# A decoder trunk on one core: the first norm's weight as one row, and a written order for the first projection

## The chip, the cores and the metric

One core of a Trainium2 chip runs the whole program. The metric is the device time of one execution in microseconds (us); lower is better. TensorE (PE), VectorE (DVE), ScalarE (ACT), GpSimd (POOL) and SyncE (SP) each run their own list of instructions in order; SP issues nearly all the transfers (DMA).

## What is computed

Two layers on 256 tokens of width 1024, in float32. Layer 0 has stick-breaking heads and differential heads side by side, layer 1 has sparse attention, and each is followed by a squared-ReLU MLP. Every sub-layer starts with an RMS norm:

```python
def rmsnorm(x, g):
    x32 = x.astype(jnp.float32)
    y = x32 * lax.rsqrt(jnp.mean(x32 * x32, axis=-1, keepdims=True) + RMS_EPS)
    return (y * g.astype(jnp.float32)).astype(x.dtype)

proj = h @ w_in                       # h = rmsnorm(x, attn_norm[0])
sb_q, sb_k, sb_v, df_q, df_k, df_v = jnp.split(proj, 6, axis=-1)
```

The change concerns the very first of these norms and the projection `sb_v` behind it.

## The kernel before

The 256 tokens are two halves of 128 rows (`t` = 0 and 1), one token to a partition, 1024 columns in two parts of 512 (`n`). Matrix products need the width on the partitions, so a normed half (tile `xg`) is transposed by PE in pieces of 128x128 into `ps_t`, four to a PSUM bank.

To keep float32 accuracy at the fast product type, every operand is the sum of a high and a low part: the high part is a cast on ACT (`x0h` of the activations, `wh` of the weights), the low part is what the cast lost, a subtraction on DVE (`x0l`, `wl`). Each product is then three: high with high, low with high, high with low.

The class `Weights` streams the matrices. One entry of its list is 1 MB and comes in two loads of 512 KB (tile `w`, `load`, L48, issued by SP); `split` (L56) casts and subtracts each half. There are four load buffers (`RAW`), so the fifth load waits until DVE or POOL has read the first. The first entry is `sbv` 0 (rows 0 to 511 of the `sb_v` columns), the second `sbv` 1 (rows 512 to 1023), then `sbq` 0, `sbk` 0 and so on. For `sbv` 1 the subtraction is on POOL (`ON_POOL`, L38).

`run` (L1059) starts with the loads of x for token half 0 (two of 256 KB), the norm's weight, three weight halves, x for token half 1, a fourth weight half. `load_gain` (L243) brings the norm's weight to all partitions by a DMA that reads one row 128 times (512 KB). `identities` runs 13 products on zeros on PE ahead of the real work (`ps_warm`). `norm_full` (L297) then squares on ACT (L253), multiplies x by -0.5 and the weight on DVE (L294), forms the reciprocal root from logarithm and exponential on ACT and two small DVE operations (L258), multiplies `xg` by it (L309) and transposes. `constants` (L124) prepares small matrices on POOL and casts four of them on DVE. The first projection is `project_v` (L492): for token half 0 and then for token half 1, 24 products of 128x512 each. Behind it `halves` computes q and k of the first heads (`ps_f`, two entries, 96 products of 128x256), and then come the attention scores `z`.

The order of the instructions of an engine is set by a scheduler that places them when the program is built, from the order of the code; nothing pins it here.

Of the kernel before, what the change touches and what calls it, by code (L numbers as in the profile page):

```python
# [22 lines left out]
KT = D // P  # L23
EPS = 1e-6
# [8 lines left out]
class Weights:  # L33
# [1 line left out]


    RAW, SPLIT, BUFS = 4, 1, 4
    ON_POOL = [("sbv", 1)]  # L38

    def __init__(self, nc, pool):  # L40
        self.nc, self.pool = nc, pool
# [12 lines left out]
        self.raw.append(w)  # L54

    def split(self):  # L56
        i = len(self.ready)
        a, b = self.todo[i][1].shape[1:]
        n = a * b
        wh, wl = (self.pool.tile([P, 2048], F32R, tag=k, name=f"{k}{i}", bufs=self.BUFS) for k in ("wh", "wl"))  # L60
        for j in range(2):
            while len(self.raw) <= 2 * i + j:
                self.load()
            w = self.raw[2 * i + j]
            c = slice(j * n // 2, (j + 1) * n // 2)
            self.nc.scalar.copy(wh[:, c], w)  # L66
            key = self.todo[i][0]
            eng = self.nc.gpsimd if key in self.ON_POOL else self.nc.vector
            eng.tensor_sub(wl[:, c], w, wh[:, c].bitcast(F32))  # L69
        self.ready.append(tuple(t[:, :n].rearrange("p (a b) -> p a b", b=b) for t in (wh, wl)))  # L70

    def prefetch(self):
        while len(self.ready) < min(self.n_used + self.SPLIT + 1, len(self.todo)):
# [12 lines left out]
class Trunk:  # L86
# [18 lines left out]
        return self.psum.tile([P, 512], F32, tag="B", name=name, bufs=4)  # L105

    def mm(self, out, lhsT, rhs, start, stop, **kw):
        self.nc.tensor.matmul(out, lhsT, rhs, start=start, stop=stop, **kw)  # L108


    def identities(self):
        nc, c = self.nc, self.const
        self.ident = c.tile([P, P], F32, name="ident")
        make_identity(nc, self.ident)
        self.identb = c.tile([P, P], BF16, name="identb")
        nc.vector.tensor_copy(self.identb, self.ident)

        zero = c.tile([P, 512], BF16, name="zero")
        nc.vector.memset(zero, 0.0)
        ps = self.bankB("ps_warm")  # L120
        for i in range(13):
            self.mm(ps, zero[:, :P], zero, i == 0, i == 12)

    def constants(self):  # L124
        nc, c = self.nc, self.const

        u = c.tile([P, P], F32, name="u")
        nc.gpsimd.memset(u, -1.0)
        nc.gpsimd.affine_select(out=u, in_=u, pattern=[[-1, P]], compare_op=ALU.is_ge,
                                fill=0.0, base=0, channel_multiplier=1)  # L130
        self.negU = c.tile([P, P], F32R, name="negU")
        nc.vector.tensor_copy(self.negU, u)
        n1 = c.tile([P, P], F32, name="n1")
        nc.gpsimd.memset(n1, -1.0)
        self.neg1 = c.tile([P, P], F32R, name="neg1")
        nc.vector.tensor_copy(self.neg1, n1)

        m = c.tile([P, P], F32, name="m")
        nc.gpsimd.memset(m, 0.0)
        nc.gpsimd.affine_select(out=m, in_=m, pattern=[[1, P]], compare_op=ALU.is_gt,  # L140
                                fill=NEG, base=0, channel_multiplier=-1)
        self.maskb = c.tile([P, P], BF16, name="maskb")
        nc.vector.tensor_copy(self.maskb, m)
# [98 lines left out]

    def load_gain(self, row):  # L243
        self.gain = self.tmp.tile([P, D], F32, tag="gain", name="gain")
        self.nc.sync.dma_start(self.gain, row.partition_broadcast(P))

    def square_half(self, t, n):

# [6 lines left out]
        self.v = v  # L255
        return v

    def rsqrt(self, v):  # L258
# [3 lines left out]
        nc.scalar.activation(u, v, AF.Ln)  # L262
        nc.scalar.activation(y, u, AF.Exp, scale=-0.5)
        if v.shape[1] == 1:
            nc.vector.scalar_tensor_tensor(o, y, y, v, op0=ALU.mult, op1=ALU.mult)
        else:
            nc.vector.tensor_mul(o, y, y)
            nc.vector.tensor_mul(o, o, v)
        nc.vector.scalar_tensor_tensor(r, o, -3.0, y, op0=ALU.add, op1=ALU.mult)
        return r  # L270

    def split_psum(self, hi, lo, src):
# [214 lines left out]
    def even_mixer(self, xT, oT, pool, out):  # L487
        nc = self.nc
        vsb = pool.tile([P, 2, 512], F32, name="vsb")
        vdf = pool.tile([P, 2, 512], F32, name="vdf")  # L490

        def project_v(key, dst, between=None):  # L492
            w = [self.W.get((key, 0)), None]
            pss = [self.bankB("ps_v0"), self.bankB("ps_v1")]
            self.tmajor(pss[0], w[0], xT, 0, range(4), True, False)
            w[1] = self.W.get((key, 1))
            self.tmajor(pss[0], w[1], xT, 0, range(4, 8), False, True)
            nc.scalar.copy(dst[:, 0, :], pss[0])
# [20 lines left out]
        project_v("sbv", vsb)  # L519
# [539 lines left out]
    def run(self):  # L1059
        nc, a, tc = self.nc, self.a, self.tc  # L1060
        self.rs2 = {}
        self.x = self.const.tile([P, 2, D], F32, name="x")
        self.late = []
        self.weight_order()
        nc.scalar.preload_act_table_set("natural_log_exp_and_others")
        for n in range(2):
            nc.sync.dma_start(self.x[:, 0, n * 512 : n * 512 + 512], a["x"][0][:P, n * 512 : n * 512 + 512])
        self.load_gain(a["attn_norm"][0])
        for _ in range(3):
            self.W.load()  # L1070
        nc.sync.dma_start(self.x[:, 1, :], a["x"][0][P:, :])
        self.W.load()
        self.identities()
        xT = self.new_T("x0")
        for t in range(2):
            for n in range(2):
                self.norm_full(t, n, xT)
            if t == 0:
                self.W.split()
        self.constants()  # L1080
# [90 lines left out]
```

## Time and profile before

| | |
|---|---|
| median of 3 runs | 662.26 us (661.87 to 663.5) |
| profiled execution, its own time | 662.43 us |
| its span | 660.7 us |
| PE busy | 641.3 us, 97% of the span |
| DVE, ACT, POOL busy | 62%, 52%, 7% |
| chain that ended last: PE, DVE, ACT | 90%, 5%, 2% |
| moved by DMA | 108.67 MB, 164 GB/s over the span |

The span runs from the first to the last instruction that the profiler saw. "Busy" means that an engine executed something; PE works on products, and idle time of an engine that nobody waits for costs nothing. The chain that ended last is followed backwards from the last instruction, each time to what released it, so its pieces add up to the span.

### The profile page before, as it was taken

The numbers are of one execution on the slowest core, as the hardware profiler recorded it, in microseconds if no ns is written. First come the engines' busy times: TensorE is split into PE (matmuls) and PEld (weight loads), VectorE is DVE, ScalarE is ACT, GpSimd is POOL, SyncE is SP. The second block draws the span as 40 slices with busy tenths as digits, with TensorE's granted clock in tenths as the row PEclk, the third lists the DMA queues.
The fourth block names the chain that finished last, engine by engine and source line by source line (L and its number), as shares of the span: only waits on it lengthen the run. The fifth ranks groups of instructions, "written<-read, shape, count | busy, mean of one in ns | idle before, by whom it ended". The sixth has DMA issues, their size and how long they took to land.

```text
span 660.7 us, 11136 instructions
## 1 busy us (share of the span) xinstructions
PE 641.3 (97%) x4257; PEld 562.2 (85%) x4257; DVE 407.7 (62%) x820; ACT 345.5 (52%) x699; POOL 46.3 (7%) x139
## 2 busy tenths in 40 slices
PE   6999999999999999999999899999999999999995
PEld 3799898899898989988899778777899898999984
DVE  4845577886555555555877476776765555555534
ACT  5564666464444444543567374654554444444523
POOL 2200000000000000000203231440000000000000
PEclk8899999999999999999999999999999999999999
DMA  6785243456565556664596612014365555555501
GB/s 253 226 257 157 73 176 106 156 183 208 178 182 182 186 188 192 191 191 141 173 307 208 223 64 64 23 43 156 118 214 186 182 183 181 188 189 189 192 2 64
DMA packets 74277, 108.67 MB, mean 164 GB/s; under 512 B 5072, under 2 KB 60400, under 8 KB 74224
## 3 DMA queue, kind: packets, MB, share of 16 engines
q1 hardware_dynamic: 74224, 107.97, 50.9%
q8 instruction: 33, 0.54, 0.3%
q14 instruction: 20, 0.16, 0.1%
HBM read 106.91 MB, written 1.05 MB: 163 GB/s over the span
## 4 chain that ended last, share of the span: by engine, by line
PE 90%; DVE 5%; ACT 2%; issue 1%; DMA 1%; SPq 0%; ACTq 0%; DVEq 0%
PE macc L108 27%; PE ps_up L108 24%; PE ps_f L108 7%; PE acc L108 5%; PE ps_q L108 4%; PE ps_ut L108 3%; PE ps_v L108 2%; PE o L108 2%; PE s L108 2%; PE ps_or L108 2%; PE ps_k L108 2%; PE pt L1026 2%; DVE wl L69 2%; PE z L108 1%; PE ps_h L108 1%
## 5 line engine op out<-in xcount | busy, mean ns | idle before, releaser
L69 DVE TENSOR_TENSOR wl<-w,wh 128x1024 fp32r<-128x1024 f32 (+1 forms) x188 | 224.9, 1214 | 166.1 <-ACT wh L66 165.6
L66 ACT CAST wh<-w 128x1024 fp32r<-128x1024 f32 (+1 forms) x190 | 192.9, 1040 | 172.7 <-PE macc L108 83.3
L108 PE MATMUL macc<-wh,l 128*128 128x512 f32 x256 | 101.2, 395 | 0.0
L108 PE MATMUL macc<-wh,h 128*128 128x512 f32 x256 | 101.1, 395 | 0.0
L108 PE MATMUL macc<-wl,h 128*128 128x512 f32 x256 | 101.0, 394 | 0.0
L108 PE MATMUL ps_up<-m0h,wh 128*128 128x256 f32 x224 | 63.5, 283 | 0.0
L108 PE MATMUL ps_up<-m1h,wh 128*128 128x256 f32 x224 | 63.5, 283 | 0.0
L108 PE MATMUL ps_up<-m0h,wl 128*128 128x256 f32 x224 | 63.4, 283 | 0.0
L108 PE MATMUL ps_up<-m1h,wl 128*128 128x256 f32 x224 | 63.3, 283 | 0.0
L108 PE MATMUL ps_up<-m1l,wh 128*128 128x256 f32 x224 | 63.3, 283 | 0.0
L108 PE MATMUL ps_up<-m0l,wh 128*128 128x256 f32 x224 | 63.3, 283 | 0.0
L108 PEld LDWEIGHTS macc<-wh,l 128*128 128x128 f32 x256 | 48.2, 188 | 11.1
L108 PEld LDWEIGHTS macc<-wh,h 128*128 128x128 f32 x256 | 48.4, 189 | 10.0
L108 PEld LDWEIGHTS macc<-wl,h 128*128 128x128 f32 x256 | 48.3, 189 | 10.0
L108 PEld LDWEIGHTS ps_up<-m0l,wh 128*128 128x128 f32 x224 | 42.9, 191 | 0.6
L108 PEld LDWEIGHTS ps_up<-m1l,wh 128*128 128x128 f32 x224 | 42.9, 191 | 0.6
L108 PEld LDWEIGHTS ps_up<-m1h,wh 128*128 128x128 f32 x224 | 42.9, 191 | 0.6
L108 PEld LDWEIGHTS ps_up<-m0h,wh 128*128 128x128 f32 x224 | 42.9, 191 | 0.6
L108 PEld LDWEIGHTS ps_up<-m1h,wl 128*128 128x128 f32 x224 | 42.9, 191 | 0.0
L108 PEld LDWEIGHTS ps_up<-m0h,wl 128*128 128x128 f32 x224 | 42.9, 191 | 0.0
L983 POOL TENSOR_SCALAR p<-p,sums 128x128 f32<-128x128 f32 (+1 forms) x64 | 31.4, 508 | 80.5 <-ACT kd L720 25.8
L108 PE MATMUL ps_f<-x0h,wh 128*128 128x256 f32 x128 | 36.5, 285 | 0.0
(285 smaller groups left out, 1191.2 us busy)
## 6 DMA issues: line engine op xcount, KB each, us to landing
w<-in_mlp_w_dram SPq DMA_DIRECT2D x128, 512.0 KB, 4.3
w<-in_ev_w_in_dram SPq DMA_DIRECT2D x24, 512.0 KB, 4.8
w<-in_od_w_in_dram SPq DMA_DIRECT2D x18, 512.0 KB, 5.0
w<-in_ev_w_out_dram SPq DMA_DIRECT2D x8, 512.0 KB, 4.3
w<-in_od_w_out_dram SPq DMA_DIRECT2D x8, 512.0 KB, 3.6
cwk<-in_od_cmp_k_w_dram SPq DMA_DIRECT2D x8, 256.0 KB, 6.5
cwv<-in_od_cmp_v_w_dram SPq DMA_DIRECT2D x8, 256.0 KB, 5.1
w<-in_od_w_in_dram SPq DMA_DIRECT2D x4, 304.0 KB, 2.9
```

The costliest lines, as they stand in the source:

```text
L66: self.nc.scalar.copy(wh[:, c], w)
L69: eng.tensor_sub(wl[:, c], w, wh[:, c].bitcast(F32))
L108: self.nc.tensor.matmul(out, lhsT, rhs, start=start, stop=stop, **kw)
L983: nc.gpsimd.tensor_scalar(o[:, h], o[:, h], sums[:, h : h + 1], 0.0, op0=ALU.mult, op1=ALU.add)
L1026: nc.tensor.transpose(pt[:, h * P : (h + 1) * P], p[g, t, b][:, h, kt * P : (kt + 1) * P], self.ident)
```

## The change

In words, with the lines of the changed code:

- The weight of the first norm is loaded as one row of 4 KB into one partition (`g1`), by a DMA that ACT issues. PE multiplies it by a column of -0.5 in full float32 (`ps_g`, two products of 128x512 with one row of contraction), so that every partition has -0.5 times the weight in PSUM. One DVE pass then makes `xg` = x times reciprocal root times `ps_g`; the separate scaling pass is gone.
- SP loads in this order: x of token half 0, both halves of `sbv` 0, x of token half 1, both halves of `sbv` 1. The small loads of `scalars` (`lam`, `subln`) come behind the two halves of `sbq` 0, and the second norm's weight (`in_mlp_norm`) later, among the `ev_w_out` loads.
- 5 products on zeros in place of 13: four ahead of `ps_g`, one behind.
- For `sbv` 1 the high part is cast on POOL and the low part subtracted on DVE. The four casts of `constants` move from DVE to POOL, and one memset (`n1`) from POOL to DVE.
- A new function, `entry`, writes out the order of the norm and the projection for all engines and pins it; the order behind it is that of before apart from the rows that moved.

The core of the diff:

```diff
-    ON_POOL = [("sbv", 1)]
...
+    def hi(self, j, on_pool=False):
+        w, h, _ = self.half(j)
+        return (self.nc.gpsimd.tensor_copy if on_pool else self.nc.scalar.copy)(h, w)
+
+    def lo(self, j, i=None):
+        w, h, l = self.half(j, i)
+        return self.nc.vector.tensor_sub(l, w, h.bitcast(F32))
...
+        g1 = self.tmp.tile([1, D], F32, tag="xg", name="g1")
+        nc.scalar.dma_start(g1, self.a["attn_norm"][0].rearrange("(o d) -> o d", o=1))
+        nc.scalar.preload_act_table_set("natural_log_exp_and_others")
+        for n in range(2):
+            nc.sync.dma_start(self.x[:, 0, n * 512 : n * 512 + 512], self.a["x"][0][:P, n * 512 : n * 512 + 512])
+        W.open()
+        nc.sync.dma_start(self.x[:, 1, :], self.a["x"][0][P:, :])
+        for _ in range(2):
+            W.load()
+        self.identities()
...
+        self.warm(4)
+        for n in range(2):
+            keep(self.mm(ps_g[n], self.n1[:1, :], g1[:, n * 512 : n * 512 + 512], True, True))
+        self.warm(1)
...
+        def scale(t, r):
+            self.xg = self.tmp.tile([P, D], F32, tag="xg", name="xg")
+            for n in range(2):
+                c = slice(n * 512, n * 512 + 512)
+                keep(nc.vector.scalar_tensor_tensor(self.xg[:, c], self.x[:, t, c], r, ps_g[n], op0=ALU.mult,
+                                                    op1=ALU.mult))
...
+        square(0, 0)
+        square(0, 1)
+        scale(0, rs(0))
+        self.constants()
+        keep(W.hi(0))
+        keep(W.hi(1))
+        h, l0 = flip(0, 0)
+        keep(nc.scalar.copy(*h))
+        h, l1 = flip(0, 1)
+        square(1, 0)
+        keep(nc.scalar.copy(*h))
+        square(1, 1)
+        keep(W.lo(0))
+        keep(nc.vector.tensor_sub(*l0))
+        keep(W.lo(1))
+        keep(nc.vector.tensor_sub(*l1))
+        W.close()
+        scale(1, rs(1))
+        W.open()
+        for j in range(2):
+            W.hi(j, True)
+        pss = [self.bankB("ps_v0"), self.bankB("ps_v1")]
+        w = W.ready[0]
+        for j in range(3):
+            values(0, w, True, j)
+        W.close()
+        w2 = W.ready[1]
+        W.n_used = 1
+        values(0, w2, False, 0)
+        h, l0 = flip(1, 0)
+        keep(nc.scalar.copy(*h))
+        values(0, w2, False, 1)
+        h, l1 = flip(1, 1)
+        x1 = nc.scalar.copy(*h)
+        keep(x1)
+        for j in range(2):
+            keep(W.lo(j, 1))
+            keep(nc.vector.tensor_sub(*(l0, l1)[j]))
+        values(1, w, True, 0)
+        values(1, w, True, 2)
+        values(1, w2, False, 0)
+        values(0, w2, False, 2)
+        with self.tc.issue_after(x1.ins):
+            W.get(("sbv", 1))
+        keep(nc.scalar.copy(v[:, 0, :], pss[0]))
+        values(1, w, True, 1)
+        values(1, w2, False, 1)
+        values(1, w2, False, 2)
+        keep(nc.scalar.copy(v[:, 1, :], pss[1]))
...
-        nc.vector.tensor_copy(self.negU, u)
+        nc.gpsimd.tensor_copy(self.negU, u)
```

`flip` is the transposes of one part, `values(t, w, first, j)` four products of the projection: j = 0 high with high, 1 low with high, 2 high with low.

How PE's list stands at the first projection, before (`wh_150`, `wl_151` are `sbv` 0, `wh_222`, `wl_223` are `sbv` 1, `ps_v_236` and `ps_v_237` token halves 0 and 1, `wh_250` is `sbq` 0):

```order
L286 MATMUL ps_t_143<-ident,xg 128x128 x4
L108 MATMUL ps_v_236<-wh_150,x0h 128x512 x4
L108 MATMUL ps_v_236<-wh_150,x0l 128x512 x4
L108 MATMUL ps_v_236<-wl_151,x0h 128x512 x4
L108 MATMUL ps_v_236<-wh_222,x0h 128x512 x4
L108 MATMUL ps_v_236<-wh_222,x0l 128x512 x4
L108 MATMUL ps_v_236<-wl_223,x0h 128x512 x4
L286 MATMUL ps_t_273<-ident,xg 128x128 x4
L286 MATMUL ps_t_280<-ident,xg 128x128 x4
L108 MATMUL ps_v_237<-wh_150,x0h 128x512 x4
L108 MATMUL ps_f<-x0h,wh_250 128x256
```

And now (`wh_97`, `wl_98` are `sbv` 0, `wh_208`, `wl_209` are `sbv` 1, `ps_v_212` and `ps_v_213` the token halves):

```order
L191 MATMUL ps_t_183<-ident,xg 128x128 x4
L122 MATMUL ps_v_212<-wh_97,x0h 128x512 x4
L122 MATMUL ps_v_212<-wh_97,x0l 128x512 x4
L122 MATMUL ps_v_212<-wl_98,x0h 128x512 x4
L122 MATMUL ps_v_212<-wh_208,x0h 128x512 x4
L191 MATMUL ps_t_230<-ident,xg 128x128 x4
L122 MATMUL ps_v_212<-wh_208,x0l 128x512 x4
L191 MATMUL ps_t_240<-ident,xg 128x128 x4
L122 MATMUL ps_v_213<-wh_97,x0h 128x512 x4
L122 MATMUL ps_v_213<-wl_98,x0h 128x512 x4
L122 MATMUL ps_v_213<-wh_208,x0h 128x512 x4
L122 MATMUL ps_v_212<-wl_209,x0h 128x512 x4
```

The transposes of token half 1 moved from behind all 24 products of token half 0 to behind 16 of them, and three groups of token half 1 stand ahead of the last group of token half 0.

How DVE's list stands at the first norm of the two token halves, before:

```order
L294 SCALAR_TENSOR_TENSOR xg<-x,gain 128x512 x2
L309 TENSOR_SCALAR xg<-xg,rs_129 128x512 x2
L116 CAST identb<-ident 128x128
L69 TENSOR_TENSOR wl_151<-w_79,wh_150 128x1024
L274 TENSOR_TENSOR x0l<-ps_t_136,x0h 128x4x128
L274 TENSOR_TENSOR x0l<-ps_t_143,x0h 128x4x128
L132 CAST negU<-u 128x128
L69 TENSOR_TENSOR wl_151<-w_81,wh_150 128x1024
L294 SCALAR_TENSOR_TENSOR xg<-x,gain 128x512 x2
```

And now, to the start of the second one's scaling:

```order
L184 SCALAR_TENSOR_TENSOR xg<-x,rs_133,ps_g_114 128x512
L184 SCALAR_TENSOR_TENSOR xg<-x,rs_133,ps_g_115 128x512
L80 TENSOR_TENSOR wl_98<-w_93,wh_97 128x1024
L216 TENSOR_TENSOR x0l<-ps_t_177,x0h 128x4x128
L80 TENSOR_TENSOR wl_98<-w_95,wh_97 128x1024
L218 TENSOR_TENSOR x0l<-ps_t_183,x0h 128x4x128
L175 TENSOR_SCALAR v_125<-ss_124 128x1
L176 SCALAR_TENSOR_TENSOR v_125<-ss_124,v_125 128x1
L394 SCALAR_TENSOR_TENSOR rs_199<-rs_197,v_125 128x1
L398 SCALAR_TENSOR_TENSOR rs_200<-rs_199,rs_197 128x1
L184 SCALAR_TENSOR_TENSOR xg<-x,rs_200,ps_g_114 128x512
```

Two passes over `xg` became one, the casts of constants are gone from between, and the weight subtractions alternate with those of `x0l`.

## Rows read from the trace of the kernel before

**Rows 1.** Page, part 1: busy time of each engine over the span.
```profile
PE 641.3 (97%) x4257; PEld 562.2 (85%) x4257; DVE 407.7 (62%) x820; ACT 345.5 (52%) x699; POOL 46.3 (7%) x139
```

**Rows 2.** Chain that ended last, 0 to 60 us: start us, us, what.
```profile
1.72 7.29 DMA gain<-in_attn_norm_dram
...
9.11 1.29 DVE xg L294 x2
...
15.63 5.65 DVE xg L294 x2
...
26.42 4.81 PE ps_v L108 x20
31.23 11.29 PE ps_f L108 x94
42.52 0.02 issue
42.55 1.04 ACT wh L66
```

**Rows 3.** Loads at the start: SP's issues (start us, us), then size and us to landing.
```profile
2.18 1.46 SPq L53 DMA_DIRECT2D w<-in_ev_w_in_dram  x3
...
4.81 1.46 SPq L53 DMA_DIRECT2D w<-in_ev_w_in_dram  x1
...
w<-in_ev_w_in_dram SPq DMA_DIRECT2D x1, 512.0 KB, 8.2
...
w<-in_ev_w_in_dram SPq DMA_DIRECT2D x1, 512.0 KB, 10.9
...
w<-in_ev_w_in_dram SPq DMA_DIRECT2D x24, 512.0 KB, 4.8
...
lam<-in_ev_lam_q_dram SPq DMA_DIRECT2D x2, 0.2 KB, 4.3
```

**Rows 4.** Timeline, 4 to 6 us: start us, us, engine, line, operation.
```profile
4.23 0.63 ACT L253 ACTIVATE sq<-x 128x512 bf16<-128x512 f32 x1
...
4.76 0.19 ACT L253 ACTIVATION_READ_ACCUMULATOR sq<-x 128x1 f32 x1
...
5.96 0.16 DVE L269 SCALAR_TENSOR_TENSOR rs<-rs,rs 128x1 f32<-128x1 f32 x1
```

**Rows 5.** Groups of instructions by shape, 0 to 31 us: busy us, mean ns | idle before.
```profile
L66 ACT CAST wh<-w 128x1024 fp32r<-128x1024 f32 x10 | 10.2, 1047 | 7.1 <-DMA w<-in_ev_w_in_dram 7.1
L69 DVE TENSOR_TENSOR wl<-w,wh 128x1024 fp32r<-128x1024 f32 x7 | 8.4, 1223 | 0.4 <-ACT wh L66 0.2
L294 DVE SCALAR_TENSOR_TENSOR xg<-x,gain 128x512 f32<-128x512 f32 x4 | 6.9, 1775 | 3.0 <-DMA gain<-in_attn_norm_dram 3.0
...
L69 POOL TENSOR_TENSOR wl<-w,wh 128x1024 fp32r<-128x1024 f32 x2 | 5.2, 2642 | 11.0 <-ACT wh L66 11.0
...
L274 DVE TENSOR_TENSOR x0l<-ps_t,x0h 128x512 fp32r<-128x512 f32 x4 | 2.7, 688 | 0.2 <-ACT x0h L273 0.2
...
L273 ACT CAST x0h<-ps_t 128x512 fp32r<-128x512 f32 x4 | 2.2, 588 | 0.9 <-PE ps_t L286 0.9
```

**Rows 6.** Timeline of PE: the products on zeros, first and second transposes, float32 products.
```profile
1.25 5.73 PE L108 MATMUL ps_warm<-zero 128*128 128x512 bf16 x13 [1.25 <-DVE zero L119]
...
23.25 1.07 PE L286 MATMUL ps_t<-ident,xg 128*128 128x128 f32 x8 [0.64 <-DVE xg L309]
...
106.00 0.94 PE L108 MATMUL odf<-vdf,df_a 128*128 128x128 f32 x6 [0.16 <-DVE df_a L650]
```

**Rows 7.** Stretches: length, PE PEld DVE ACT POOL busy, granted clock, DMA share, GB/s.
```profile
8.00:10.00 2.00, 0.00 (x0) 0.00 (x0) 0.90 (x2) 0.00 (x0) 0.00 (x0) 1.00 1.04 394
...
18.00:20.00 2.00, 2.00 (x6) 1.53 (x5) 2.00 (x2) 0.00 (x0) 2.00 (x1) 0.50 0.69 202
...
22.00:24.00 2.00, 1.36 (x10) 0.95 (x9) 1.77 (x5) 2.00 (x4) 0.00 (x0) 1.00 0.76 239
```

**Rows 8.** Timeline of POOL in layer 1: passes with one tensor input, 256 columns, by fours.
```profile
363.31 3.85 POOL L983 TENSOR_SCALAR p<-p,sums 128x256 f32<-128x256 f32 x4 [2.79 <-DVE sums L981]
...
417.08 1.84 POOL L983 TENSOR_SCALAR p<-p,sums 128x256 f32<-128x256 f32 x4 [1.65 <-DVE sums L981]
```

More of the change, by code (lines that the diff above doesn't have):

```diff
@@ L56, in split, with open, half, close @@
     def split(self):
+        self.open()
+        for j in range(2):
+            self.hi(j)
+            self.lo(j)
+        self.close()
+    def open(self):
         i = len(self.ready)
+        while len(self.raw) <= 2 * i + 1:
+            self.load()
         a, b = self.todo[i][1].shape[1:]
[L59 to L70, printed above, removed]
+        self.n = a * b
+        self.hl = [self.pool.tile([P, 2048], F32R, tag=k, name=f"{k}{i}", bufs=self.BUFS) for k in ("wh", "wl")]
+    def half(self, j, i=None):
+        c = slice(j * self.n // 2, (j + 1) * self.n // 2)
+        return self.raw[2 * (len(self.ready) if i is None else i) + j], self.hl[0][:, c], self.hl[1][:, c]
+    def hi(self, j, on_pool=False):
[4 more added lines that the diff above has]
+        return self.nc.vector.tensor_sub(l, w, h.bitcast(F32))
+    def close(self):
+        b = self.todo[len(self.ready)][1].shape[2]
+        self.ready.append(tuple(t[:, : self.n].rearrange("p (a b) -> p a b", b=b) for t in self.hl))
     def prefetch(self):
@@ L107, in mm @@
     def mm(self, out, lhsT, rhs, start, stop, **kw):
-        self.nc.tensor.matmul(out, lhsT, rhs, start=start, stop=stop, **kw)
+        return self.nc.tensor.matmul(out, lhsT, rhs, start=start, stop=stop, **kw)
     def identities(self):
@@ L114, in identities @@
         make_identity(nc, self.ident)
[L115 to L122, printed above, removed]
+        self.zero = c.tile([P, 512], BF16, name="zero")
+        nc.vector.memset(self.zero, 0.0)
+        self.n1 = c.tile([P, P], F32, name="n1")
@@ new lines, in identities, with keep, warm, entry @@
+        nc.vector.memset(self.n1, -0.5)
+    def keep(self, *todo):
+        for ins in todo:
+            self.tc.keep_in_program_order(ins)
+    def warm(self, n):
+        for i in range(n):
+            self.keep(self.mm(self.ps_warm, self.zero[:, :P], self.zero, i == 0, i == n - 1))
+    def entry(self, dst, v, banks):
+        nc, W, keep = self.nc, self.W, self.keep
+        g1 = self.tmp.tile([1, D], F32, tag="xg", name="g1")
[8 more added lines that the diff above has]
+        self.identities()
+        self.ps_warm = banks.tile([P, 512], F32, name="ps_warm")
+        ps_g = [banks.tile([P, 512], F32, name=f"ps_g{n}") for n in range(2)]
+        self.warm(4)
+        for n in range(2):
+            keep(self.mm(ps_g[n], self.n1[:1, :], g1[:, n * 512 : n * 512 + 512], True, True))
+        self.warm(1)
+        sq = self.tmp.tile([P, 512], BF16, tag="sq", name="sq", bufs=1)
+        ss = self.sm.tile([P, 4], F32, tag="ss4", name="ss4", bufs=1)
+        ms = self.sm.tile([P, 2], F32, tag="v2", name="v2", bufs=1)
+        def square(t, n):
+            keep(nc.scalar.activation(sq, self.x[:, t, n * 512 : n * 512 + 512], AF.Square,
+                                      accum_out=ss[:, 2 * t + n : 2 * t + n + 1]))
+        def rs(t):
+            o = ms[:, t : t + 1]
+            keep(nc.vector.tensor_scalar(o, ss[:, 2 * t : 2 * t + 1], 1.0 / D, EPS, op0=ALU.mult, op1=ALU.add))
+            keep(nc.vector.scalar_tensor_tensor(o, ss[:, 2 * t + 1 : 2 * t + 2], 1.0 / D, o, op0=ALU.mult,
+                                                op1=ALU.add))
+            return self.rsqrt(o, keep)
+        def scale(t, r):
[4 more added lines that the diff above has]
+                                                    op1=ALU.mult))
+        def flip(t, n):
+            ps = self.bankB(f"ps_t{t}{n}")
+            for i in range(4):
+                kt = 4 * n + i
+                keep(nc.tensor.transpose(ps[:, i * P : (i + 1) * P], self.xg[:, kt * P : (kt + 1) * P], self.ident))
+            z = ps.rearrange("p (k c) -> p k c", c=P)
+            hi, lo = (d[:, 4 * n : 4 * n + 4, t * P : (t + 1) * P] for d in dst)
+            return (hi, z), (lo, z, hi.bitcast(F32))
+        def values(t, w, first, j):
+            ps, kts, tq = pss[t], range(4 * (not first), 4 * (not first) + 4), slice(t * P, (t + 1) * P)
+            x, y = ((dst[0], w[0]), (dst[1], w[0]), (dst[0], w[1]))[j]
+            for i, kt in enumerate(kts):
+                keep(self.mm(ps, x[:, kt, tq], y[:, i], first and i == j == 0, not first and j == 2 and i == 3))
+        square(0, 0)
[33 more added lines that the diff above has]
+        keep(x1)
+        for j in range(2):
+            keep(W.lo(j, 1))
[11 more added lines that the diff above has]
+        keep(nc.scalar.copy(v[:, 1, :], pss[1]))
@@ L124, in constants @@
     def constants(self):
         nc, c = self.nc, self.const
+        self.identb = c.tile([P, P], BF16, name="identb")
+        nc.gpsimd.tensor_copy(self.identb, self.ident)
         u = c.tile([P, P], F32, name="u")
@@ L131, in constants @@
         self.negU = c.tile([P, P], F32R, name="negU")
-        nc.vector.tensor_copy(self.negU, u)
-        n1 = c.tile([P, P], F32, name="n1")
-        nc.gpsimd.memset(n1, -1.0)
+        nc.gpsimd.tensor_copy(self.negU, u)
         self.neg1 = c.tile([P, P], F32R, name="neg1")
-        nc.vector.tensor_copy(self.neg1, n1)
+        nc.gpsimd.tensor_scalar(self.neg1, self.n1, 2.0, 0.0, op0=ALU.mult, op1=ALU.add)
         m = c.tile([P, P], F32, name="m")
@@ L142, in constants @@
         self.maskb = c.tile([P, P], BF16, name="maskb")
-        nc.vector.tensor_copy(self.maskb, m)
+        nc.gpsimd.tensor_copy(self.maskb, m)
         dist = c.tile([P, 2 * P + 2 * CW], F32, name="dist")
@@ L244, in load_gain @@
         self.gain = self.tmp.tile([P, D], F32, tag="gain", name="gain")
-        self.nc.sync.dma_start(self.gain, row.partition_broadcast(P))
+        self.tc.keep_in_program_order(self.nc.sync.dma_start(self.gain, row.partition_broadcast(P)))
     def square_half(self, t, n):
@@ L256, in square_half, with rsqrt @@
         return v
-    def rsqrt(self, v):
+    def rsqrt(self, v, keep=lambda ins: None):
         nc = self.nc
         y, u, o, r = (self.sm.tile(list(v.shape), F32, tag=f"rs{i}", name=f"rs{i}") for i in range(4))
-        nc.scalar.activation(u, v, AF.Ln)
-        nc.scalar.activation(y, u, AF.Exp, scale=-0.5)
+        keep(nc.scalar.activation(u, v, AF.Ln))
+        keep(nc.scalar.activation(y, u, AF.Exp, scale=-0.5))
         if v.shape[1] == 1:
-            nc.vector.scalar_tensor_tensor(o, y, y, v, op0=ALU.mult, op1=ALU.mult)
+            keep(nc.vector.scalar_tensor_tensor(o, y, y, v, op0=ALU.mult, op1=ALU.mult))
         else:
@@ L268, in rsqrt @@
             nc.vector.tensor_mul(o, o, v)
-        nc.vector.scalar_tensor_tensor(r, o, -3.0, y, op0=ALU.add, op1=ALU.mult)
+        keep(nc.vector.scalar_tensor_tensor(r, o, -3.0, y, op0=ALU.add, op1=ALU.mult))
         return r
@@ L518, in even_mixer @@
         ksb = pool.tile([P, 4, S], F32, tag="k", name="ksb")
-        project_v("sbv", vsb)
+        with self.tc.tile_pool(name="ps_in", bufs=1, space=PSUM) as banks:
+            self.entry(xT, vsb, banks)
         halves(0, "sbq", "sbk", qsb, ksb)
@@ L1064, in run @@
         self.weight_order()
[L1065 to L1073, printed above, removed]
-        xT = self.new_T("x0")
[L1075 to L1080, printed above, removed]
+        xT = self.new_T("x0")
         for l in range(2):
```

## The prediction
> **What bounds the kernel now.** First the page: PE is busy for 97% of the span [rows 1]. Whatever this change is worth has to come from places where PE waits, and it touches the start alone, so the second view is the chain that ended last, for the first 60 us [rows 2]. Three pieces of it are no PE work. From 1.72 to 9.0 the chain hangs on the load of the norm's weight. At 9.1 DVE starts on the first `xg`. At 15.6 the two `xg` passes of token half 1 take 5.65 us, where the same two took 1.29 us at 9.1; in between POOL ran the two `sbv` 1 subtractions of 2.64 us each [rows 5], and the DVE passes ended only with them. From 26.4 on the chain is PE without a break: 20 `ps_v` products, then 94 of the 96 `ps_f` products from 31.2 (two ran earlier, so as if from 31.0), up to a short wait for ACT at 42.5. From 31.0 on the two programs carry the same work on PE in the same order. So the question is one number: when does the `ps_f` stream start?
>
> **The loads.** Five loads of 512 KB stand behind the gain. The first of them was issued at 2.18 and landed 8.2 us later, at 10.4; the last was issued at 4.81 and landed after 10.9, at 15.7 [rows 3]. Four more transfers in 5.3 us is 1.33 us for each. Token half 0 of x is there by 4.2, when its second square starts [rows 4]; from 4.2 to 10.4 are 6.2 us for two transfers, so the gain cost about 4.9 us of queue instead of 1.33. Taken out, with the new order, the landings become: `sbv` 0 at 5.5 and 6.9, x of token half 1 at 8.2, `sbv` 1 at 9.5 and 10.9.
>
> **The gain as a product.** The 4 KB row is ACT's first issue, at about 0.8 (SP's two loads of x stand ahead of the gain's at 1.72, at some 0.45 each). The trace has no load on that queue. Above, the tiny `lam` loads take 4.3 us [rows 3]: landing at 5.1. Below, x itself: its first part is there when the first square starts, 0.82 ahead of 4.23, at 3.4 [rows 4]. I take 3.4, since nothing stands in front of it. A float32 product has its nearest row in `odf`: six of 128 columns in 0.94 us, 0.157 us each at the high clock [rows 6]; four times the columns at half the clock is 1.25 us, for two 2.5 us. Below, a product on zeros costs 5.73/13 = 0.44 us. With 2.5 us `ps_g` is ready at 5.9. The reciprocal root, untouched by the change, is ready at 5.96 + 0.16 = 6.1 [rows 4]: that is the cover, and the weight costs nothing. Without it (landing at 5.1) the first scale starts at 7.6, 1.5 us later, and everything behind it moves along.
>
> The page "FP8 and Floating Point Precision" of the Trainium skill, section "TensorE Precision Notes", has true FP32 make four passes through the array. By it the two products would cost 2 x 4 x 0.44 = 3.5 us, an estimate, `ps_g` would come at 6.9, and 0.8 us of the gain below would go; no row here is a float32 product of 512 columns with one row of contraction.
>
> **Token half 0.** Two passes of 512 columns with one operand in PSUM cost what `x0l` costs, 0.69 us [rows 5]: 6.15 to 7.5. ACT in its written order: cast of the first `sbv` 0 half at 5.7, of the second when it lands, 6.9 to 7.95 (1.05 each), then `x0h` to 8.6 (0.59), a square to 9.4 (0.63 + 0.19 [rows 4]; x landed at 8.2), `x0h` to 10.0, a square to 10.8. PE can start on the projection at 8.6. DVE: `wl` 7.5 to 8.75 (1.22), `x0l` to 9.45, `wl` to 10.65, `x0l` to 11.35.
>
> **Token half 1.** The small operations between the second square and the reciprocal root took from 4.95 to 6.1, so 1.2 us [rows 4]: 12.6. First scaled part at 13.3. From there PE has, by its list, four transposes (0.54, half of the eight in 1.07 [rows 6]), one group of four products (20 in 4.81 us, so 0.96 a group [rows 2]), four transposes, seven groups: 0.54 + 0.96 + 0.54 + 6.72 = 8.8. **`ps_f` could start at 22.1, 8.9 us earlier than now.** The four casts of constants leave DVE and join POOL, which at present idles 11 us ahead of its subtractions [rows 5]; that idle time covers them, and their users are the scores behind 42.5. The memset on DVE runs while it waits for x. The DVE subtraction of `sbv` 1 comes back to DVE, but behind the scale, where PE has 2.04 us and more of other work ahead of it.
>
> **What I add.** POOL now casts the high part of `sbv` 1, and PE's fourth group needs it. Nearest rows: POOL passes with one tensor input over four times 256 columns, 1.84 us undisturbed and 3.85 us beside DVE work [rows 8]. From the landing at 9.5: done at 13.2 (below, PE 0.4 us late) or 17.2 (above, 4.4 us late). DVE in turn has one `wl` at 9.45, which can be held as the `xg` passes were, by up to one cast (1.84). I take 1.2 us in all, nearer the undisturbed row, because just one large DVE pass with two SBUF operands falls into that time. Start of `ps_f`: 23.3, gain 7.7 us. Against the profiled execution's 662.43 us that is 654.7; the median of the runs stands 0.17 below, so the forecast is **654.5 us**.
>
> A rule that bears on this: "GPSIMD Engine Reference", section "Key points", in the Trainium skill has POOL share its SBUF interfaces with VectorE, with contention for VectorE instructions that have two SBUF inputs. The 5.65 us agree. By it the new scale, with one operand in PSUM, would not be held at all, and the sum would be 653.3 if nothing else is late; no run here shows that yet.
>
> **The weights behind.** `sbk` 0 loads into the buffers of `sbv` 1, so its first half is issued after DVE's subtraction at 15.3 + 1.2 = 16.5, behind the five small loads, and lands 4.8 us later [rows 3], at 21.3; cast and subtraction follow within 2.3, the second half about 2 us behind. PE needs it at 23.3 + 48 x 0.12 = 29.1. Cover: about 3.5 us; beyond that each us late costs one. The second norm's weight moves among loads whose weights are two entries ahead of PE: nothing.
>
> **The rivals.**
> - *Nothing held* (0.18): POOL and DVE don't meet, `ps_f` at 22.1, 653.3 us. For it: DVE's list is the longest of the three here. Against it: 5.65 us for 1.29 in the trace.
> - *Held longer* (0.28): POOL at the disturbed price, 4.4 us late: gain 4.5, 657.8 us. The clock belongs here: the granted clock was at the high level in the idle stretch 8 to 10, at the low one (1.2 GHz) at 18 to 20 though PE was busy throughout, and high at 22 to 24 [rows 7]. With 5 products on zeros for 13 and gaps behind them, PE may run the first four groups at the low level, 1.76 for 0.96 each: 3.2 us, of which the waits for POOL and DVE swallow at least half.
> - *The stream runs dry* (0.06): the start is as forecast, but `sbk` 0 lands late behind five small loads; 6 us late beyond its cover gives 660.5.
> - *It does not reach the end* (0.05): something that I don't see binds at 31 in both, for example the buffers at four loads; 662.
> - *Slower* (0.03): the clock stays at the low level into `ps_f`. There a us of stream loses half a us, so after the start at 23.3 it takes 15.4 us at 1.2 GHz, to 39, to use up the 7.7; from then on the kernel is slower, 665 at some 44. For it: at 18 to 20 PE was busy throughout and still at the low level [rows 7]. Against it: it was high two us later, and the `ps_f` stream is unbroken.
>
> **How the numbers follow.** Forecast 0.40, the others as given. Faster by over 0.3% (2 us, what a measurement of this kernel can tell from no change): 0.40 + 0.18 + 0.28 + most of the dry case = 0.91; within: 0.05; slower: 0.04. The range goes from a little under the bare sum, 652.4, to the two upper bounds together (gain 8.9 - 4.4 - 1.5 = 3.0), 659.3.
>
> **What would show it.** The first scale on DVE near 6.2, not at 9.1; the first `x0h` near 8.0; the second scale 1.4 us for two and near 12.6 to 14; `ps_f` unbroken from 22 to 25, and the rest of the span as before, shifted. Wrong: `ps_g` ready after 7.6, POOL casts over 3 us each, PE at the low clock after 15, or a wait for DMA inside the first 96 `ps_f` products.

## The result, and the profile after

| | before | after |
|---|---|---|
| median of the runs | 662.88 us (661.87 to 664.64) | 654.25 us (653.99 to 654.64) |
| profiled execution, own time | 662.43 us | 654.64 us |
| its span | 660.7 us | 652.9 us |

The ratio after to before is 0.9868, 95% interval 0.9848 to 0.9887. The forecast was 654.5. The number came out; the way to it did not, as the rows show. Two executions of 1250 us, one of the kernel before and one of the 32-byte kernel below, are left out of the ranges and ratios. First the page of the changed kernel:

```profile
span 652.9 us, 11125 instructions
...
PE 637.6 (98%) x4253; PEld 561.1 (86%) x4253; DVE 404.1 (62%) x815; ACT 344.1 (53%) x697; POOL 44.8 (7%) x142
```

PE has 3.7 us less busy time than in [rows 1], so the 7.8 us of span are not waits alone. The chain that ended last, 0 to 60 us, of the changed kernel (start us, us, what):

```profile
2.84 6.34 DMA w<-in_ev_w_in_dram
...
9.20 1.05 ACT wh L76
10.25 0.49 ACT x0h L210
...
10.79 6.19 PE ps_v L122 x16
...
24.05 5.88 DMA w<-in_ev_w_in_dram
...
30.00 1.06 ACT wh L76
...
31.09 1.24 DVE wl L80
...
32.34 4.59 DMA w<-in_ev_w_in_dram
...
37.03 1.04 ACT wh L76
38.08 0.29 ACT ksb L640
...
38.41 1.48 PE z L122 x16
39.89 11.55 PE ps_f L122 x96
```

Against [rows 2] the load of the norm's weight and the two long `xg` passes are gone. The loads of the weight matrices stand in their place, twice: the second half of `sbv` 0, which lands at 9.18 and holds the start, and from 24 to 37 the weights of the `ps_f` stream. The last pieces matter: the scores `z` wait for the copy `ksb`, and on ACT that copy stands behind the cast of a weight that landed at 36.93.

PE's timeline (start us, us, engine, line, operation; in brackets the idle time before and what ended it):

```profile
3.13 3.75 PE L122 MATMUL ps_g<-g,n 1*128 1x512 f32 x4
...
10.79 2.08 PE L122 MATMUL ps_v<-wh,x0h 128*128 128x512 f32 x4 [1.04 <-ACT x0h L210]
12.66 1.91 PE L122 MATMUL ps_v<-wh,x0l 128*128 128x512 f32 x4
14.37 1.68 PE L122 MATMUL ps_v<-wl,x0h 128*128 128x512 f32 x4
15.88 1.09 PE L122 MATMUL ps_v<-wh,x0h 128*128 128x512 f32 x4
...
25.01 0.28 PE L122 MATMUL ps_f<-x0h,wh 128*128 128x256 f32 x1
```

The two products of `ps_g` take 3.75 us. The projection starts at 10.79, and its first three groups take 1.7 to 2.1 us each, where the next takes 1.09. `ps_f` starts at 25.0; before it ran as if from 31.0 [rows 2].

The scale passes on DVE, the casts of `sbv` 1 on POOL, and ACT's first cast of a weight (same columns):

```profile
6.91 1.41 DVE L184 SCALAR_TENSOR_TENSOR xg<-x,rs,ps_g 128x512 f32<-128x512 f32 x2 [0.45 <-PE ps_g L122]
...
14.71 1.41 DVE L184 SCALAR_TENSOR_TENSOR xg<-x,rs,ps_g 128x512 f32<-128x512 f32 x2
...
11.86 2.61 POOL L76 CAST wh<-w 128x1024 fp32r<-128x1024 f32 x2 [6.50 <-DMA w<-in_ev_w_in_dram]
...
7.82 1.04 ACT L76 CAST wh<-w 128x1024 fp32r<-128x1024 f32 x1 [1.81 <-DMA w<-in_ev_w_in_dram]
```

Now the same places further on, in both. The chain of the kernel before at the second pair of scores, at the first MLP, at a projection of layer 1, and at the last pass:

```profile
43.92 1.48 PE z L108 x16
...
154.07 5.58 PE macc L108 x24
...
367.51 3.11 PE ps_q L108 x24
...
656.49 0.72 ACT fin L1112
```

And of the changed kernel (its `z` is the row at 38.41 above):

```profile
148.56 5.50 PE macc L122 x24
...
360.86 3.10 PE ps_q L122 x24
...
648.69 0.72 ACT fin L1227
```

The lead is 5.51 us at `z`, still 5.51 at the first MLP, 6.65 in layer 1 and 7.80 at the end. (The profiles of the two kernels that were taken again below put `z` at 43.71 before and at 37.72 to 37.96 after, so the lead at `z` is 5.3 to 6.2 us.) So 2.3 of the 7.8 us come long after the last changed instruction, in the two MLPs, where PE runs the same products in the same order: a group of 24 `macc` products takes 5.50 us for 5.58. The study therefore had two questions: where do these 2.3 us come from, and which part of the change made the 5.5.

### The profile page after: what moved, and what is told of

Read it like the earlier page. It is cut to its first block, busy times and chain, and to the rows that moved or that the text cites. A ratio compares the mean times of both kernels' runs of the same rounds, so it can differ in the third digit from the quotient of the medians.

```text
span 652.9 us, 11125 instructions
## 1 busy us (share of the span) xinstructions
PE 637.6 (98%) x4253; PEld 561.1 (86%) x4253; DVE 404.1 (62%) x815; ACT 344.1 (53%) x697; POOL 44.8 (7%) x142
## 4 chain that ended last, share of the span: by engine, by line
PE 89%; DVE 4%; DMA 3%; ACT 2%; issue 1%; SPq 0%; ACTq 0%; DVEq 0%
PE macc L122 26%; PE ps_up L122 25%; PE ps_f L122 5%; PE acc L122 5%; PE ps_q L122 4%; PE ps_ut L122 3%; PE ps_v L122 3%; DMA w<-in_ev_w_in_dram 3%; PE o L122 2%; PE s L122 2%; DVE wl L80 2%; PE ps_or L122 2%; PE ps_k L122 2%; PE pt L1156 2%; PE z L122 1%
## 5 line engine op out<-in xcount | busy, mean ns | idle before, releaser
L80 DVE TENSOR_TENSOR wl<-w,wh 128x1024 fp32r<-128x1024 f32 (+1 forms) x190 | 227.3, 1214 | 163.3 <-ACT wh L76 163.1
```

The costliest lines, as they stand in the source:

```text
L80: return self.nc.vector.tensor_sub(l, w, h.bitcast(F32))
```

## The experiments

### Where the 2.3 us in the MLPs come from

The change adds two small tiles to the pool `sm`, `ss4` and `v2`. Every tile that is placed behind them, among them the MLP's `h` and `l`, which PE reads in `macc`, then lies 64 bytes further in each partition. The theory: this shift alone sets the pace of `macc`. The rival: something of the new entry lives on (the clock, the order of loads).

**The kernel before, once more**, on the chip of the next three.

> The kernel before, once more, for its profile on this chip. In the two profiles that were shown, the change reaches the first scores 5.5 us earlier, and the other 2.3 us come drop by drop from the second MLP products (macc, 27 groups of 24 products of 128x512): 5.58 us a group before, 5.50 in the changed kernel. If the place of the tiles in SBUF sets this pace, macc is at 5.58 us a group here again. If it is the chip or the execution, it is near 5.50 here, and the changed kernel on this chip is then 5.5 us faster than this and no more.

Measured: 662.22 us in one execution (median of before on that chip: 663.2), `macc` 5.58 us a group, `z` at 43.71. It repeats.

**The kernel before with 64 unused bytes.**

```diff
-        self.rs2 = {}
+        self.rs2, self.pad = {}, self.sm.tile([P, 16], F32, tag="pad", name="pad", bufs=1)
```

> The kernel before with 64 unused bytes at the end of the pool of small tiles, so that every tile allocated behind it (the MLP's h and l among them) lies at the address that it has in the changed kernel; the instructions and their order are those of before. If the place sets the pace of macc: 5.50 us a group, and 2.3 us off the time (ratio 0.9965). If the chip or the execution sets it: the time of before, ratio 1.000 within 0.002, and macc as in the run of before on this chip.

Measured: 659.72 us (658.31 to 660.46), ratio 0.9941 (0.9923 to 0.9959).

**The changed kernel with its two tiles in old places**, so that all else lies where it lay before.

```diff
-        ss = self.sm.tile([P, 4], F32, tag="ss4", name="ss4", bufs=1)
-        ms = self.sm.tile([P, 2], F32, tag="v2", name="v2", bufs=1)
+        ss = self.sm.tile([P, 4], F32, tag="nm", name="ss4")
+        ms = self.sm.tile([P, 4], F32, tag="sums", name="v2")
```

> The changed kernel with its two new small tiles put into buffers that exist anyway, so that every later tile lies where it lay before the change; the instructions and their order are those of the changed kernel. If the place sets the pace of macc: 5.58 us a group, and the gain shrinks to 5.5 us (some 657 us). If the chip or the execution sets it: the time of the changed kernel, 654.3 us.

Measured: 657.5 us (657.11 to 658.22), ratio 0.9911 (0.9897 to 0.9926).

**The changed kernel, once more**, beside it.

> The changed kernel again, on the chip of the three others. Both theories: about 654.3 us; if the place sets the pace, macc at 5.50 us a group here while the kernel before has 5.58 on the same chip; if not, both have the same.

Measured: 653.97 us (653.55 to 655.06), ratio 0.9859 (0.9842 to 0.9877), `macc` 5.50.

The chain of the padded kernel before, then of the changed kernel with the old places:

```profile
154.43 5.50 PE macc L108 x24
```

```profile
147.84 5.58 PE macc L122 x24
...
371.68 4.52 PE ps_q L122 x23
```

The pace follows the 64 bytes in both directions, and no instruction and no order differs within each pair. The theory stands and the rival falls: an unused tile makes the old entry's `macc` fast, and the new entry without the shift has it slow. The size is what the chains of the first two kernels gave, 2.3 us. The medians show more, 3.5 us each way. The spans of the padded pair differ by 1.7 us (660.5 and 658.8): 2.3 in the MLPs, less 0.6 that the padded kernel was late at `z` already (44.30 for 43.71). In the changed kernel's pair 1.5 us of that is one piece: the `ps_q` products at 371.68 take 4.52 us for 23, where the changed kernel takes 3.02. That piece turns up again below; why the padded pair's medians differ by more than its profiles is not explained.

**A shift by 32 bytes only** (only `ss4` goes to an old place).

```diff
-        ss = self.sm.tile([P, 4], F32, tag="ss4", name="ss4", bufs=1)
+        ss = self.sm.tile([P, 4], F32, tag="nm", name="ss4")
```

> The changed kernel with every tile behind the small ones 32 bytes lower, which is 32 bytes above where it lay before the change; the same instructions. The place sets the pace of macc (5.58 us a group at offset 0, 5.50 at offset 64). If the pace goes step by step with the offset: between the two, 654.3 to 656.6 us. If what counts is how the tiles stand to a boundary of 64 or 128 bytes (offset 0 is 96 bytes past one of 128, offset 64 is 32, and this one stands on it): a third pace, faster than 5.50 and the time below 653.

Measured: 658.21 us (655.67 to 659.96), ratio 0.9941 (0.9925 to 0.9958), `macc` 5.60 us, and the slow `ps_q` piece too. So 0, 32 and 64 bytes give 5.58, 5.60 and 5.50 us. What the good offsets have in common, and which of the moved tiles counts, is open: three offsets were tried, and all the tiles move together.

### What the row instead of the full load is worth

The weight comes again as the 512 KB load behind x, the scale reads `gain` from SBUF, and 13 products on zeros stand for the row's (the factor -0.5 goes into the reciprocal root by a small operation); all else is the changed kernel.

```diff
-        g1 = self.tmp.tile([1, D], F32, tag="xg", name="g1")
-        nc.scalar.dma_start(g1, self.a["attn_norm"][0].rearrange("(o d) -> o d", o=1))
...
+        self.load_gain(self.a["attn_norm"][0])
...
-        self.warm(4)
-        for n in range(2):
-            keep(self.mm(ps_g[n], self.n1[:1, :], g1[:, n * 512 : n * 512 + 512], True, True))
-        self.warm(1)
+        self.warm(13)
...
-                keep(nc.vector.scalar_tensor_tensor(self.xg[:, c], self.x[:, t, c], r, ps_g[n], op0=ALU.mult,
+                keep(nc.vector.scalar_tensor_tensor(self.xg[:, c], self.x[:, t, c], r, self.gain[:, c], op0=ALU.mult,
```

> The changed kernel with the row product undone: the weight comes to all partitions by one 512 KB load behind x of token half 0, as before; 13 products on zeros in place of 5 and the two of the row; one small DVE operation more for each reciprocal root. If the load's place in the queue is what the row saves: the loads of sbv 0 land 2.6 us later than in the changed kernel (10.4 and 11.7 in place of 7.8 and 9.1), the first scale starts at 9.0, the first scores come 2.6 us later, some 656.9 us; up to 1 us more if POOL's casts hold the second scale, which now has two SBUF operands. If the load is hidden behind the weights: 654.3 us.

Measured: 657.3 us (656.6 to 658.17), ratio 0.9934 (0.9916 to 0.9952). Its chain:

```profile
2.66 8.03 DMA w<-in_ev_w_in_dram
...
40.20 1.48 PE z L122 x16
...
373.01 4.53 PE ps_q L122 x23
```

The weight that holds the start lands at 10.69; in the profiled executions of the changed kernel it was there by 8.5 to 9.2. `z` starts 1.8 to 2.5 us later than in those (37.7 to 38.4). So the row, with the fewer products on zeros and the one small operation less that go with it, is worth about 2.2 us at the entry. The other 1.5 us is again the slow `ps_q` piece.

This kernel also settles what the slow first groups are. Its stretches (length; PE, PEld, DVE, ACT, POOL busy; granted clock, DMA share, GB/s), and PE at 14.16:

```profile
14.00:16.00 2.00, 2.00 (x6) 1.52 (x6) 1.36 (x5) 0.41 (x2) 1.97 (x2) 0.50 0.75 218
...
20.00:22.00 2.00, 2.00 (x13) 1.65 (x12) 1.99 (x3) 1.22 (x2) 0.00 (x0) 1.00 0.85 258
...
14.16 1.91 PE L122 MATMUL ps_v<-wh,x0l 128*128 128x512 f32 x4
```

A group of four takes 1.91 us at a granted clock of 0.50, the low level (1.2 GHz). The changed kernel's groups at 12.66 take the same 1.91, though its own row for that stretch reads 1.00:

```profile
12.00:14.00 2.00, 2.00 (x7) 1.54 (x6) 1.41 (x4) 0.86 (x4) 2.00 (x2) 1.00 0.72 207
```

By this pace it ran at the low level until 15.65, and the record of the clock does not show it.

### The low level: five more products on zeros

```diff
-        self.warm(1)
+        self.warm(2)
...
+        self.warm(4)
```

(one more behind `ps_g`, four between the second transposes and the first group)

> The changed kernel with five more products on zeros, one behind the row's products and four behind the transposes of token half 0, so that PE has no gap before the projection; only PE's list differs. If PE's pace in the projection (0.43 us a product against 0.23) sets the start of the scores: the high level comes sooner, ps_f starts up to 1.5 us earlier and the time falls by 1 to 1.5 us, to about 653. If the scores wait for a weight load that lands at 36.9 whatever PE does: ps_f starts earlier, the scores do not, and the time is 654.3 us within 0.5.

Measured: 656.88 us (653.41 to 658.84), ratio 0.9912 (0.9883 to 0.9941). PE's timeline:

```profile
12.04 1.08 PE L122 MATMUL ps_v<-wh,x0l 128*128 128x512 f32 x4
...
38.12 1.54 PE L122 MATMUL z<-qsb,ksb 64*128 64x256 f32 x8 [1.10 <-ACT ksb L641]
```

The groups run at the high level from the second on, and `ps_f` starts at 23.6. In the three profiles of the changed kernel it starts at 25.0, 23.9 and 23.8, because PE came to the high level at different times there: the third group took 1.68, 1.09 and 1.17 us. From PE's first group to `ps_f` it is 12.7 us here and 13.4 to 14.2 there, so the low level costs this stretch 0.7 to 1.5 us. Nothing of this arrives: `z` is at 38.12 as before, waiting for `ksb`. PE waits longer ahead of `z`, and the clock falls there (granted 0.57 from 38 to 40). The chain:

```profile
38.12 2.51 PE z L122 x16
40.63 12.08 PE ps_f L122 x96
```

The same two pieces take 1.48 and 11.55 us in the changed kernel, so 1.6 us are lost here, and in layer 1 the slow `ps_q` piece costs its 1.5 us. Neither number of the expectation came: the profiled execution is 2.7 us longer than the changed kernel's (655.6 and 652.9). The low level at the entry was real, but these runs show no time that it cost the changed kernel behind `z`.

### The copy that stands behind a landing

`ksb` is put ahead of the next weight's cast in ACT's list (`last_f` is the copy of the last `ps_f` result).

```diff
-            w = [self.W.get((key, 0)), None]
+            with self.tc.issue_after(ksb0.ins):
+                w = [self.W.get((key, 0)), None]
...
+        ksb0 = self.last_f
```

> The changed kernel with one pair of ACT's instructions exchanged: the copy of the last ps_f result (ksb) stands ahead of a weight cast that waits for its load. If the scores wait for that load through ACT's order: the second pair of scores starts at about 37.0 in place of 38.4, and the time falls by 1.4 us to about 652.9. If the wait comes back at the next step (the softplus or the weights of the next projection): 654.3 us.

Measured: 653.07 us (651.32 to 654.21), ratio 0.9868 (0.9846 to 0.989). Its chain:

```profile
23.03 11.51 PE ps_f L122 x96
34.54 2.09 PE z L122 x24
36.62 11.56 PE ps_f L122 x96
```

The wait is gone: from 23.0 PE runs without a break. That `z` waited through ACT's order agrees with this and with the chain above. What the exchange is worth in time is not shown. The ratio of the medians is that of the changed kernel (0.9868), and the profiled execution is the fastest of the four (651.32 us). In it ACT's first cast of a weight, which the edit does not touch, ran at 5.91, where the profiles of the changed kernel have it at 7.21 to 7.82:

```profile
5.91 1.03 ACT L76 CAST wh<-w 128x1024 fp32r<-128x1024 f32 x1
```

Then both together, and **the changed kernel a third time** on the same chip.

> The changed kernel once more, as the measure for the three beside it. From its two earlier measurements: 653.5 to 655 us, ratio to the kernel before 0.985 to 0.988. The second pair of scores z starts at 38.0 to 38.5 us, the macc groups of 24 products take 5.50 us. If the stretch of products at the low level near 371 us (1.5 us, seen in four other executions and not in this kernel's two) goes with an execution and not with a kernel, it may show here too, and then the time is 655 to 656.

Measured: 653.72 us (653.42 to 655.45), ratio 0.9872 (0.9848 to 0.9896); `z` at 37.72, second `ps_f` at 39.19, no slow piece at 370. Its chain:

```profile
37.72 1.48 PE z L122 x16
```

> The changed kernel with the copy of ksb ahead of the weight's cast on ACT, and with five more products on zeros in PE's list. Theory: two waits lie one behind the other. The zeros alone brought ps_f 1.3 us forward and were stopped at z, which waited for ksb behind a cast that waited for a load; the copy alone takes that stop away. Together the earlier start reaches the end: ps_f at 23.0 to 23.9, z without a wait at 34.5 to 35.5 (38.0 to 38.5 in the changed kernel), time 650.5 to 652, 2 to 3.5 us under the changed kernel beside it. Rival: the loads set the pace as soon as the copy no longer does, and PE then waits for a weight inside the ps_f stream or runs z at the low level: z at 37 or later, 653 to 655, no better than the changed kernel.

Measured: 653.3 us (652.55 to 654.79), ratio 0.9862 (0.984 to 0.9884). ACT's timeline, and the chain:

```profile
34.43 1.05 ACT L76 CAST wh<-w 128x1024 fp32r<-128x1024 f32 x1 [0.46 <-DMA w<-in_ev_w_in_dram]
...
35.82 2.13 PE z L122 x24
37.95 11.56 PE ps_f L122 x96
```

`z` starts 1.9 us earlier, but has 24 products left where the changed kernel has 16, so the stream behind it is 1.24 us ahead; the spans differ by 1.3 (650.9 and 652.2). The medians differ by 0.4 us, with ranges that overlap. A wait is left, as the rival had it: both copies of `ksb` still stand behind the cast at 34.43, whose weight had just landed, and PE waits 0.36 us for them ahead of `z`. The expectation of 2 to 3.5 us is refuted; that this version beats the changed kernel is not shown.

### POOL and DVE back in their old roles for `sbv` 1

```diff
-            W.hi(j, True)
+            keep(W.hi(j))
+            W.lo(j, None, True)
...
-            keep(W.lo(j, 1))
```

(`lo` with `True` subtracts on POOL.)

> The changed kernel with sbv 1 as in the kernel before: high part by ACT, low part subtracted by POOL. POOL's two subtractions then lie from 12.9 to 18.2 us, over DVE's second scale of xg at 14.4 to 15.8, whose operands are x in SBUF and ps_g in PSUM. Theory (the page on GpSimd of the Trainium skill: contention for VectorE instructions with two SBUF inputs): this scale is not held and takes 1.4 us for two as in the changed kernel; the buffers of sbv 1 come free at about 15.5 and 18.2 instead of 17 and 18.8, so the loads behind come a little earlier: 652.5 to 654.5. Rival: POOL's subtractions hold every DVE pass that touches SBUF, as they did 5.65 us for two before: the scale ends at 18 to 20, ps_f and z come 2 to 4 us later, 656 to 658.

Measured: 654.62 us (653.83 to 654.84), ratio 0.9877 (0.9861 to 0.9892). DVE and POOL, and the chain at `z`:

```profile
14.30 1.41 DVE L184 SCALAR_TENSOR_TENSOR xg<-x,rs,ps_g 128x512 f32<-128x512 f32 x2
...
14.84 4.75 POOL L80 TENSOR_TENSOR wl<-w,wh 128x1024 fp32r<-128x1024 f32 x2 [9.48 <-ACT wh L76]
...
38.69 1.48 PE z L122 x16
```

The second pass of the scale, from 15.0, lies wholly beside POOL's subtraction, and the two still take 1.41 us, not the 5.65 of [rows 2]. One operand in PSUM instead of two in SBUF is enough; the swap of roles was not what freed the scale. The rule of the Trainium skill ("GPSIMD Engine Reference", "Key points") names contention for VectorE instructions with two SBUF inputs. These 1.41 us agree with it. The loads behind did not come earlier as had been expected, since POOL ended at 19.6 and not at 18.2. `z` starts at 38.69, 0.97 us later than in the changed kernel beside it (37.72); 0.5 of that is there at PE's first group already (10.62 for 10.12), behind a landing that the edit does not touch. The swap is worth 0.5 to 1 us.

### x of token half 1 in its old place

```diff
-        W.open()
-        nc.sync.dma_start(self.x[:, 1, :], self.a["x"][0][P:, :])
-        for _ in range(2):
+        for _ in range(3):
             W.load()
+        nc.sync.dma_start(self.x[:, 1, :], self.a["x"][0][P:, :])
+        W.load()
+        W.open()
```

> The changed kernel with x of token half 1 loaded behind three weight halves, as before, instead of two. Theory of the chain: it lands at 11.4 to 11.8 instead of 10.1 to 10.5, the squares, the second scale (14.4 to 14.7 now) and DVE's subtractions of sbv 1 behind it go with it, the loads into those buffers too, and z with its ksb: all about 1.3 us later, second scale at 15.8 to 16.1, z at 39.3 to 39.8, 655 to 656. Rival: the slow start of PE has slack there and the third weight half, now there 1.3 us earlier, makes up for it: z at 38.0 to 38.5 and 654 as now.

Measured: 656.18 us (655.71 to 656.71), ratio 0.9901 (0.9883 to 0.992). ACT's first square of the half, and the chain at `z`:

```profile
12.78 0.63 ACT L170 ACTIVATE sq<-x 128x512 bf16<-128x512 f32 x1 [1.06 <-DMA x<-in_x_dram]
...
40.29 1.48 PE z L122 x16
```

x lands at 12.7, where in the changed kernel beside it the same square ran at 9.97; the second scale starts at 16.4 instead of 14.1, and `z` 2.57 us later. The theory of the chain holds, at double the size: x lost 2.8 us and not the 1.3 of one load. The first `sbv` 0 half came 1.6 us later too (ACT's cast at 8.83 for 7.21), which the order alone does not explain.

**The 5.5 us, by single undoings:** the row 2.2, the place of x 2.6, the roles of POOL and DVE 0.5 to 1: 5.3 to 5.8. They need not add, and the first landings alone scatter by 0.7 us between executions, but they are of the size that the chains show. The merged scale pass and the written order of the rest were not undone by themselves.

## Why the prediction came out, step by step

**The number stood on two errors that cancel.** The entry gave 5.5 us, not 7.7. The statement that from 31.0 on the two programs carry the same work on PE was true of the instructions and false of their time: 2.3 us came from where the tiles lie. The sum, 7.8, looks like the forecast. That the median lies 0.25 us from it is luck.

- **The loads: spacing right, origin wrong.** They follow each other at 1.3 us as forecast. The first landed at 7.8 (ACT's first cast follows at once), not 5.5. The failed step is "the gain cost about 4.9 us of queue": the same load landed at 10.4 before, so the gain cost 2.6 there, and 1.5 to 2.2 in the kernel that brings it back. The kernel with x late has the load order of before without the weight's load, and its first half landed at 8.8: that leaves 1.6 of the 2.6 for the load itself. The idle time between x and the first weight had been put down to the gain whole. The landing also differs between executions: in the profile of the kernel with `ksb` ahead it had come by 5.9.
- **The row as a product: price wrong, verdict right.** 3.75 us for the two, not 2.5. The estimate from the four passes of the Trainium skill ("FP8 and Floating Point Precision", "TensorE Precision Notes") was 3.5 us. The measured 3.75 us is nearer to it than to the 2.5. But the higher price took nothing of the gain. The first scale waited 0.45 us for `ps_g`, and the chain does not go through it: `x0h` stood on ACT behind the second weight cast, whose load landed at 9.18. The late loads were the cover.
- **PE's start** was at 10.8, not 8.6, by these loads.
- **The low level** was counted in a rival only. It held to 15.65 in this profile. By the kernel with more zeros it cost the stretch up to `ps_f` 0.7 to 1.5 us, and by `z` nothing of that is left.
- **POOL and DVE: 1.2 us added, 0.2 measured.** POOL's casts took 1.3 us each, under both bounds (1.84 and 3.85): four small passes were no fit row for a long one. In the kernel with x late, where none began within a subtraction of DVE's, they took 1.04. No large DVE pass was held, not even the subtraction with two SBUF operands at 11.38 (1.22 us). One small operation was: the first of the two behind the root for token half 1 (128x1, at 14.03) took 0.45 us beside POOL's second cast, against 0.22 for token half 0, and the second scale waits for it. The rival "nothing held" had this nearly right, at another start.
- **`ps_f`** so started at 25.0: 22.1 bare, 2.1 for the loads, 1.5 for the level (14.2 us from PE's first group in this profile, 12.7 with more zeros), less 0.7 in other places; forecast 23.3.
- **The weights behind.** The cover of 3.5 us was worked out for one entry. The chain from 24 to 37 is a ring instead: landing, cast, subtraction, next load into the freed buffer. It took 0.5 us of the 6.0 through `ksb`. The rival "the stream runs dry" named the resource, but it bit at `z`, through ACT's order, not inside `ps_f`.
- **Slower, or no effect at the end:** neither came.

## What to carry to other kernels

A gain at the start is worth only what the next wait lets through: follow the chain past the place of the change, and look there for a copy that stands in an engine's list behind an instruction that waits for a load. When a change adds or drops even a small tile, compare the pace of products far from it, and test a suspected difference by an unused tile of the same size. A forecast that hits the number is judged by its steps: measure the lead at several places along the program, not at the end alone.

## What the runs showed of the hardware that was not expected

- 64 bytes of offset of later tiles changed a group of 24 `macc` products from 5.58 to 5.50 us, and 32 bytes gave 5.60; `ps_up` stayed at 5.75 throughout.
- In four of the profiled executions (old places, 32 bytes, full load, five zeros) 23 `ps_q` products near 372 us took 4.5 us for 3.0. In the full-load kernel the granted clock there is 0.50:

```profile
374.00:376.00 2.00, 2.00 (x11) 2.00 (x11) 1.77 (x8) 1.04 (x5) 0.00 (x0) 0.50 0.23 79
```

  In the other profiled executions, the changed kernel's three among them, it did not happen. The wait of 0.79 us ahead of the products is the same there as in the changed kernel. It is 1.5 us of the differences between medians above. The mean granted clock of all executions points to the execution, with odds that differ by kernel: with five more zeros it read 0.993 or 0.994 in four (656.80 to 658.84 us) and 0.998 in two (653.41 and 655.03 us), with 32 bytes 0.994 in four of nine, and in the twelve of the changed kernel 0.995 to 0.998. That each low reading is this stretch is not shown, and what decides it stays open.
- The granted clock of a stretch can read 1.00 while every product takes the time of the low level; the pace of known products is the safer witness.
